# Remainders of the first difference tiles on GpSimd, and three more seven-product pairs, in an encoder layer

## The chip, the cores and the metric

The kernel runs on one core of one Trainium2 chip. The metric is the time of one execution in device microseconds; a time is a median over runs. The engines are named as in the profile: PE is TensorE (matmuls), DVE is VectorE, ACT is ScalarE, POOL is GpSimd, SP issues most DMAs.

## The reference

One layer of a bidirectional encoder in float32, for 256 tokens of width 4096:

```
h    = rms_norm(x, g_mix)
proj = h @ w_in                      # 4096 -> 11840: q, kv latents, rotary key, gates, dilated q, k, v
y_a  = rms_norm(mla_attention(...))     * silu(gate_a)      # 16 heads, latents through w_uq, w_ukv
y_b  = rms_norm(dilated_attention(...)) * silu(gate_b)      # 16 heads, three dilation patterns
x    = x + concat(y_a, y_b) @ w_out                          # 4096 -> 4096
gate = sigmoid(rms_norm(x, g_ple) @ w_ple_gate)              # 4096 -> 4096
x    = x + (p @ w_ple) * gate
out  = rms_norm(x, g_final)
```

Nearly all of the work is three large products: 256 x 4096 by 4096 x 11840, and twice 256 x 4096 by 4096 x 4096.

## The kernel before

**A product in three matmuls.** Every float32 operand is held as a high part in the fast float32 format and a remainder. ACT copies the source into `hi` (which rounds), and DVE subtracts: `lo = src - hi`. That is the helper `split`. A product `a b` is then three matmuls, `hi hi`, `hi lo`, `lo hi` (the helper `mm`). Each weight tile that is loaded must so be split before PE can use it; the left sides are split once.

**Blocks.** A `Block` computes 256 tokens by 1024 columns of one weight over a depth of 4096, which is 32 rows of tiles, called kt here. There are 18 of them: six dilated ones (`w_in`: q, k, v of heads 0 to 7, then of heads 8 to 15), five gate blocks (the first holds the q latent, the others `gate_b` and `gate_a`), three of `w_out`, four of `w_ple_gate` (the fourth leaves its last 8 kt to a closing part). Between them lie the kv latents, the attention heads and the half chunks of `w_out`, which have no pairs.

**Plain steps and pairs.** A plain step (`plain_step`) takes one kt: one load of 128x1024, one split of 128x1024 (ACT and DVE once each), four products of 128x512 (two token tiles by two column halves). A pair of kt can be done instead by a scheme of the Strassen kind with seven products for eight (`fast_steps`, kind "f" in the order of steps). It needs sums of the left side, made once by DVE (`add_sums`), and four differences of weight tiles, which DVE makes for each pair: `T[0]` (two of 128x512: the first difference tiles) and, from it, `T[1]`. A pair is four steps: "M1" (a half split, one product), "M2 M3" (a split of the second raw tile, two products), "M5 M7" (a split of `T[0]`, two products) and "M6 M4" (a split of `T[1]`, two products). So a pair costs DVE four differences of 128x512, one remainder of 128x512 and three of 128x1024.

**How many pairs.** Tables of numbers set the pairs in each block: `FAST_QKV`, `FAST_G`, `FAST_O`, `FAST_P`. The function `spread` lays the steps of a block out: some plain steps ahead (`LEAD_...`), some behind, and between them pairs and plain steps mixed by the DVE cost that a table gives each step:

```
FAST_COST, PLAIN_COST, PLAIN_TIME = (1.8, 2.3, 1.15, 1.15), 1.15, 2.73
FAST_TIME = 0.69, 1.37, 1.37, 1.37
```

At a block's end DVE adds the eight PSUM banks into the block's result: `d_mid` and `d_done` in the dilated blocks, with 11 instructions of 128x512 that read PSUM, and `gate_mid`, `gate_done`, `out_mid`, `out_done`, `wide_mid`, `wide_done` elsewhere.

**What sets the order.** Every engine runs its instructions in the order in which the program emits them. The emitter keeps a clock of its own for each engine (`Clock`, with a cost for each kind of instruction in `Metered`) and decides by it: it converts steps (loads, splits) ahead of the product that PE is at, up to five steps, and puts conversions ahead of other work when less than `MARGIN = 4.0` us are in hand. GpSimd's cost there is

```
us = n * 0.0024 + 0.1
```

for n elements a row, and each engine's cost is taken by itself. GpSimd's own work before is the 30 sums `acc += junk` of attention (128x256, both inputs in SBUF), four DMAs and some memsets.

Of the kernel before, what the change touches and what calls it, by code (L numbers as in the profile page):

```python
# [15 lines left out]
AF = mybir.ActivationFunctionType  # L16
ALU = mybir.AluOpType
# [3 lines left out]
S = 256  # L21
# [189 lines left out]
def encoder_layer(ctx: ExitStack, tc: tile.TileContext, x, p, positions, g_mix, w_in, g_q_latent, w_uq,  # L211
# [3 lines left out]
    nc = Engines(whole, clock)  # L215
# [11 lines left out]
    def slot(tag, shape, dtype=F32):  # L227
        names[tag] = names.get(tag, 0) + 1
        return clock.made(sp.tile([P, *shape], dtype, tag=tag, name=f"{tag}_{names[tag]}"), tag)

    def bank(tag, shape, bufs=1):
        names[tag] = names.get(tag, 0) + 1
        return clock.made(pp.tile([P, *shape], F32, tag=tag, name=f"{tag}_{names[tag]}", bufs=bufs), tag, bufs)
# [8 lines left out]
    def plain(t):  # L242
        return t.bitcast(F32)

    def split(hi, lo, src, scale=None):

        if scale is None:
            nc.scalar.activation(hi, src, AF.Copy)
            nc.vector.tensor_tensor(lo, src, plain(hi), op=ALU.subtract)
        else:  # L250
            nc.scalar.activation(hi, src, AF.Copy, scale=scale)
            nc.vector.scalar_tensor_tensor(lo, src, scale, plain(hi), op0=ALU.mult, op1=ALU.subtract)
# [10 lines left out]
    def mm(ps, a, b, start, stop):  # L263

        (ah, al), (bh, bl) = a, b
        nc.tensor.matmul(ps, ah, bh, start=start, stop=False)
        nc.tensor.matmul(ps, ah, bl, start=False, stop=False)
        nc.tensor.matmul(ps, al, bh, start=False, stop=stop)
# [883 lines left out]
    class Block:  # L1152
# [62 lines left out]
        def fast_steps(self, j):  # L1215

            r, T = [], []
            (A11, A21), (A12, A22) = [[lambda k=k, t=t: tuple(q[:, t * P:(t + 1) * P] for q in self.lhs(k))
                                       for t in range(NT)] for k in (2 * j, 2 * j + 1)]
            S = lambda n: (lambda: self.sums[j][n])  # L1220

            def sub(dst, a, b):
                nc.vector.tensor_tensor(dst, a, b, op=ALU.subtract)

            def split1(hi, lo):
                if isinstance(self.tmp, tuple):
                    T.extend(slot(b, [2, self.q]) for b in self.tmp)
                else:
                    both = slot(self.tmp, [4, self.q])
                    T.extend((both[:, :2], both[:, 2:]))  # L1230
                sub(T[0][:, 0], r[0][:, 1], r[0][:, 0])
                sub(T[0][:, 1], r[0][:, 1], r[1][:, 1])
                split(hi[:, 0], lo[:, 0], r[0][:, 0])

            def split2(hi, lo):
                nc.scalar.activation(hi, r[1], AF.Copy)
                sub(T[1][:, 0], r[1][:, 1], T[0][:, 0])
                sub(T[1][:, 1], r[1][:, 0], T[1][:, 0])
                nc.vector.tensor_tensor(lo, r[1], plain(hi), op=ALU.subtract)

            def run(*which):
                def go(hi, lo):
                    for i, (m, a) in enumerate(which):
                        self.product(m, a(), (hi[:, i], lo[:, i]))
                return go

            needs = [*self.needs(2 * j), *self.needs(2 * j + 1), (self.name, j), *self.fast_needs]
            more = [*needs, *self.turn_needs]
            return [
                self.step("M1", tuple(lambda k=k: r.append(self.load(k)) for k in (2 * j, 2 * j + 1)), split1, run(("M1", A11)), needs, 1, 0.69),  # L1250
                self.step("M2 M3", None, split2, run(("M2", A12), ("M3", S(3))), needs, 1, 1.37),
                self.step("M5 M7", None, lambda hi, lo: split(hi, lo, T[0]), run(("M5", S(0)), ("M7", S(2))), more, 0, 1.37),
                self.step("M6 M4", None, lambda hi, lo: split(hi, lo, T[1]), run(("M6", S(1)), ("M4", A22)), more, 0, 1.37),
            ]

# [94 lines left out]
    pT, ple, gF, U = [], {}, [], []  # L1350
    part2 = [[stat(1) for _ in range(4)] for _ in range(NT)]
    FAST, WIDE, LAST_K = 7, 4, 8
    FAST_P, LEAD_P, TRAIL_P = (7, 7, 7, 5), (6, 6, 6, 4), (4, 4, 4, 4)
    HALVES = (0, S), (S, Q)
    PLE_AT = 0, 3
    HURRY, REST, QUIET = -4, 0, 3
# [334 lines left out]
    G_BANKS = "m2", "m3", "s", "o", "m0", "m1", "t0", "t1"  # L1691
    H_BANKS = "m0", "m1", "t0", "t1", "m2", "m3", "s", "o"
    Y_BANKS = "s", "o", "t0", "t1", "m0", "m1", "m2", "m3"
    FAST_QKV, LEAD_QKV = (3, 7, 8, 8, 8, 7), (18, 4, 4, 4, 4, 4)
    FAST_G, LEAD_G = (3, 6, 7, 7, 7), (15, 10, 6, 6, 4)
    LEAD_L = LEAD_G[0]
    E_BANKS = "m2", "m3", "m0", "m1", "s", "o", "t0", "t1"
# [60 lines left out]
    for n, (dil, half) in enumerate(((None, 0), (1, 0), (1, 1), (0, 0), (0, 1))):  # L1758
        hook(len(steps), only(*(("t0", "t1"), ("m0", "m1"))[n % 2]))
        order = spread(FAST_G[n], LEAD_G[n], 4)  # L1760
        lo = {None: 0, 0: OFF_GA, 1: OFF_GB}[dil] + 1024 * half
# [120 lines left out]
    def tick():  # L1882

        advance(spare=slack(ran[0] + 1) > MARGIN)
# [4 lines left out]
    class Old(Step):  # L1889
# [18 lines left out]
        def run(self, hi, lo):  # L1908
            ch, j = self.ch, self.j
            if j == 0:  # L1910
                ch.ps = {t: bank(ch.banks[t], [512]) for t in ch.ts}
                locks.update(self.banks)
            for k in range(ch.per):
                kt = ch.per * j + k
                a = ch.lhs(kt)
                for t in ch.ts:
                    mm(ch.ps[t][:, :ch.n], tuple(q[:, t * P:(t + 1) * P] for q in a), (hi[:, k], lo[:, k]),
                       kt == 0, kt == ch.nk - 1)
                    tick()
            if ch.per * (j + 1) == ch.nk:  # L1920
                self.after = lambda: ch.done(Sums({t: q[:, :ch.n] for t, q in ch.ps.items()}, ch.banks))
# [156 lines left out]
```

## Time and profile before

| | before |
|---|---|
| time, median of 3 runs (lowest, highest) | 1900.3 us (1899.37, 1900.38) |
| the profiled execution | 1899.12 us, span 1897.4 us |
| granted TensorE clock | 0.998 |
| PE busy | 1878.5 us, 99% |
| DVE busy | 1696.8 us, 89% |
| ACT busy | 1140.2 us, 60% |
| POOL busy | 31.2 us, 2% |
| read from HBM | 364.72 MB, 194 GB/s over the span |

Busy is the time in which an engine has at least one instruction under way. In the profile's rows a line is nearly always L177, that of the helper through which every instruction is emitted; the tiles tell what a row is. `lo<-T,hi` or `B<-T,B` is a remainder of a difference tile (the tiles that hold splits change: `hi` and `lo`, `B`, `T`, `B7a` and `B7b`, `Ah`, `Al`); `lo<-raw,hi` is one of a loaded tile; `T<-raw,T` a difference. Digits of buffers are left out.

### The profile page before, as it was taken

How to read it: one execution, taken by the hardware profiler on the slowest of the kernel's cores; microseconds unless marked ns; L12 is line 12 of the kernel's file. 1: busy time of each engine (PE TensorE's matmuls, PEld its weight loads, DVE VectorE, ACT ScalarE, POOL GpSimd, SP SyncE). 2: the span in 40 equal slices, each digit the busy share in tenths (PEclk: the TensorE clock that was granted, in tenths of full speed). 3: DMA queues.
4: the chain of work that ended last, by engine and by line, in shares of the span. 5: the costliest groups of instructions: out<-in, count | busy, mean ns of one | idle time of the engine just before them, and what ended most of it. 6: DMA issues, size and time to landing. Idle time of an engine off the chain costs nothing.

```text
span 1897.4 us, 25417 instructions
## 1 busy us (share of the span) xinstructions
PE 1878.5 (99%) x9133; PEld 1579.8 (83%) x9133; DVE 1696.8 (89%) x2354; ACT 1140.2 (60%) x1543; POOL 31.2 (2%) x41
## 2 busy tenths in 40 slices
PE   9999999999999999999999999999999999999997
PEld 7888888888899888888888999888888888888885
DVE  6999999899898989999998777999989989989897
ACT  7655656565588555556556556656655555666654
POOL 0000000000011000000000010100000000000000
PEclk9999999999999999999999999999999999999999
DMA  8666666666735566666667553576666666665665
GB/s 279 189 205 213 214 212 200 198 213 193 218 84 159 166 211 183 196 215 189 208 199 209 137 142 123 167 231 204 216 199 217 187 194 218 194 223 183 221 222 180
DMA packets 160871, 370.59 MB, mean 195 GB/s; under 512 B 29116, under 2 KB 70952, under 8 KB 160744
## 3 DMA queue, kind: packets, MB, share of 16 engines
q1 hardware_dynamic: 159896, 366.58, 62.0%
q0 software_dynamic: 512, 1.84, 0.3%
q8 instruction: 72, 1.18, 0.3%
q10 hardware_dynamic: 336, 0.54, 0.1%
q14 instruction: 55, 0.45, 0.1%
HBM read 364.72 MB, written 4.19 MB: 194 GB/s over the span
## 4 chain that ended last, share of the span: by engine, by line
PE 85%; DVE 10%; DMA 2%; issue 2%; ACT 1%; POOL 0%; DVEq 0%; ACTq 0%; POOLq 0%
PE m L177 49%; PE t L177 16%; PE s L177 11%; PE o L177 9%; DVE lo L177 3%; DVE B L177 3%; DVE T L177 2%; DVE Ah L177 1%; DMA raw<-in_w_ple_gate_dram 1%; DVE Al L177 1%; DMA raw<-in_w_in_dram 1%; ACT hi L177 0%; DVE st L177 0%; ACT B L177 0%; DVE B7b L177 0%
## 5 line engine op out<-in xcount | busy, mean ns | idle before, releaser
L177 ACT ACTIVATE hi<-raw 128x1024 fp32r<-128x1024 f32 (+2 forms) x396 | 378.9, 966 | 278.1 <-PE m L177 70.9
L177 DVE TENSOR_TENSOR lo<-raw,hi 128x1024 fp32r<-128x1024 f32 (+2 forms) x396 | 433.4, 1107 | 61.8 <-ACT hi L177 60.6
L177 PE MATMUL m<-hi,Ah 128*128 128x512 f32 (+2 forms) x659 | 247.2, 387 | 0.3 <-ACT hi L177 0.3
L177 DVE TENSOR_TENSOR B<-raw,B 128x1024 fp32r<-128x1024 f32 (+3 forms) x228 | 213.9, 947 | 20.5 <-ACT B L177 18.8
L177 PE MATMUL m<-hi,Al 128*128 128x512 f32 (+2 forms) x625 | 229.6, 380 | 0.0
L177 PE MATMUL m<-lo,Ah 128*128 128x512 f32 (+2 forms) x549 | 207.8, 379 | 1.4 <-DVE lo L177 1.3
L177 ACT ACTIVATE B<-raw 128x1024 fp32r<-128x1024 f32 (+2 forms) x142 | 135.3, 962 | 96.8 <-DMA raw<-in_w_in_dram 25.3
L177 PE MATMUL m<-hi,B 128*128 128x512 f32 (+1 forms) x524 | 179.0, 389 | 0.0
L177 PE MATMUL m<-B,Ah 128*128 128x512 f32 (+2 forms) x554 | 146.7, 359 | 0.6 <-DVE B7b L177 0.6
L177 PEld LDWEIGHTS m<-hi,Ah 128*128 128x128 f32 x659 | 124.0, 188 | 22.7 <-ACT hi L177 1.2
L177 PEld LDWEIGHTS m<-hi,Al 128*128 128x128 f32 x625 | 117.5, 188 | 21.8
L177 PEld LDWEIGHTS m<-lo,Ah 128*128 128x128 f32 x549 | 103.4, 188 | 19.9 <-DVE lo L177 2.9
L177 PEld LDWEIGHTS m<-hi,B 128*128 128x128 f32 x524 | 98.2, 188 | 19.6
L177 PEld LDWEIGHTS m<-B,Ah 128*128 128x128 f32 x554 | 95.9, 189 | 15.3 <-DVE B7b L177 1.0
L177 PE MATMUL m<-lo,B 128*128 128x512 f32 (+1 forms) x262 | 102.1, 390 | 0.1
L177 PE MATMUL m<-B,Al 128*128 128x512 f32 (+2 forms) x289 | 99.1, 371 | 0.0
L177 DVE TENSOR_TENSOR T<-raw,T 128x512 f32<-128x512 f32 (+2 forms) x110 | 85.5, 789 | 3.3 <-ACT T L177 1.7
L177 ACT ACTIVATE hi<-B 128x1024 fp32r<-128x1024 f32 x57 | 59.4, 1056 | 23.1 <-PE m L177 7.3
L177 DVE TENSOR_TENSOR lo<-B,hi 128x1024 fp32r<-128x1024 f32 x57 | 68.5, 1220 | 3.9 <-ACT hi L177 3.6
L177 PE MATMUL t<-hi,Ah 128*128 128x512 f32 x184 | 69.9, 391 | 0.0
L177 ACT ACTIVATE B<-T 128x1024 fp32r<-128x1024 f32 (+2 forms) x55 | 50.2, 916 | 22.8 <-DVE T L177 13.4
L177 PEld LDWEIGHTS m<-B,Al 128*128 128x128 f32 x289 | 54.4, 188 | 9.2
(530 smaller groups left out, 4336.9 us busy)
## 6 DMA issues: line engine op xcount, KB each, us to landing
raw<-in_w_in_dram SPq DMA_DIRECT2D x359, 512.0 KB, 4.3
raw<-in_w_out_dram SPq DMA_DIRECT2D x128, 512.0 KB, 4.6
raw<-in_w_ple_gate_dram SPq DMA_DIRECT2D x128, 512.0 KB, 4.7
raw_q<-in_w_uq_dram SPq DMA_DIRECT2D x32, 256.0 KB, 3.8
T<-in_x_dram SPq DMA_DIRECT2D x13, 512.0 KB, 6.6
raw<-in_w_in_dram SPq DMA_DIRECT2D x16, 320.0 KB, 3.1
raw_r<-in_w_uq_dram SPq DMA_DIRECT2D x16, 256.0 KB, 4.3
raw_k<-in_w_ukv_dram SPq DMA_DIRECT2D x16, 256.0 KB, 3.4
```

The source lines that it names most:

```text
L177: return do(out, *rest, **named)
```

## The change

In the step "M5 M7" of every pair, the remainder `T[0] - hi` moves from DVE to GpSimd; ACT's copy stays. Three blocks get one pair more: the second and the sixth dilated block (7 to 8), and the fourth `w_ple_gate` block (5 to 6). There were 116 pairs, and there are 119. The cost tables of `spread` stay.

```diff
+            def split3(hi, lo):
+                nc.scalar.activation(hi, T[0], AF.Copy)
+                nc.gpsimd.tensor_tensor(lo, T[0], plain(hi), op=ALU.subtract)
+
...
-                self.step("M5 M7", None, lambda hi, lo: split(hi, lo, T[0]), run(("M5", S(0)), ("M7", S(2))), more, 0, 1.37),
+                self.step("M5 M7", None, split3, run(("M5", S(0)), ("M7", S(2))), more, 0, 1.37),
...
-    FAST_P, LEAD_P, TRAIL_P = (7, 7, 7, 5), (6, 6, 6, 4), (4, 4, 4, 4)
+    FAST_P, LEAD_P, TRAIL_P = (7, 7, 7, 6), (6, 6, 6, 4), (4, 4, 4, 4)
...
-    FAST_QKV, LEAD_QKV = (3, 7, 8, 8, 8, 7), (18, 4, 4, 4, 4, 4)
+    FAST_QKV, LEAD_QKV = (3, 8, 8, 8, 8, 8), (18, 4, 4, 4, 4, 4)
```

In the third dilated block one pair stands on DVE like this before. `T_23_2677` is its first difference tile, `T_24_2678` its second, `raw_2641` and `raw_2643` the two loaded tiles; `B_12_2706` is the remainder of a plain step that lies between:

```order
L177 TENSOR_TENSOR T_23_2677<-raw_2641 128x512
L177 TENSOR_TENSOR T_23_2677<-raw_2641,raw_2643 128x512
L177 TENSOR_TENSOR B_21_2676<-raw_2641,B_21_2676 128x512
L177 TENSOR_TENSOR T_24_2678<-raw_2643,T_23_2677 128x512
L177 TENSOR_TENSOR T_24_2678<-raw_2643,T_24_2678 128x512
L177 TENSOR_TENSOR B_21_2689<-raw_2643,B_21_2689 128x1024
L177 TENSOR_TENSOR B_12_2706<-raw_2662,B_12_2706 128x1024
L177 TENSOR_TENSOR lo_2720<-T_23_2677,hi_2719 128x1024
L177 TENSOR_TENSOR T_18_2732<-T_24_2678,T_18_2731 128x1024
```

The last row but one is the remainder of the first difference tile. A pair of the same block on DVE in the changed kernel (`T_23_2605` and `T_24_2606` are its difference tiles, `T_17_2626` and `B_14_2646` remainders of plain steps):

```order
L177 TENSOR_TENSOR T_23_2605<-raw_2575 128x512
L177 TENSOR_TENSOR T_23_2605<-raw_2575,raw_2577 128x512
L177 TENSOR_TENSOR B_20_2604<-raw_2575,B_20_2604 128x512
L177 TENSOR_TENSOR T_17_2626<-raw_2589,T_17_2625 128x1024
L177 TENSOR_TENSOR T_24_2606<-raw_2577,T_23_2605 128x512
L177 TENSOR_TENSOR T_24_2606<-raw_2577,T_24_2606 128x512
L177 TENSOR_TENSOR B_20_2635<-raw_2577,B_20_2635 128x1024
L177 TENSOR_TENSOR B_14_2646<-raw_2611,B_14_2646 128x1024
L177 TENSOR_TENSOR lo_2667<-T_24_2606,hi_2666 128x1024
```

No remainder of `T_23_2605` is left there; the row with `T_24_2606` follows at once. It stands on POOL, among those of the pairs around it:

```order
L177 TENSOR_TENSOR B_19_2522<-T_21_2476,B_19_2522 128x1024
L177 TENSOR_TENSOR lo_2586<-T_22_2542,hi_2585 128x1024
L177 TENSOR_TENSOR lo_2660<-T_23_2605,hi_2659 128x1024
L177 TENSOR_TENSOR B_21_2729<-T_24_2686,B_21_2729 128x1024
L177 TENSOR_TENSOR B_22_2792<-T_25_2748,B_22_2792 128x1024
```

POOL has one such row for each pair, one behind the other, and nothing between them in the blocks. PE reads the result in the products M5 and M7 of that pair:

```order
L177 MATMUL m_4_2514<-hi_2659,B_1_580 128x512
L177 MATMUL m_4_2514<-lo_2660,B_1_580 128x512
L177 MATMUL m_4_2514<-hi_2659,B_1_580 128x512
L177 MATMUL m_4_2518<-hi_2659,B_1_580 128x512
L177 MATMUL m_4_2518<-lo_2660,B_1_580 128x512
L177 MATMUL m_4_2518<-hi_2659,B_1_580 128x512
```

The order on PE is as before; what changes is that `lo_2660` is waited for from GpSimd.

## Prediction

> **What bounds the kernel now.** I read the page first, then the waits of PE, then the busy time of each engine block by block, and last the timeline of DVE and POOL where the two work at once.
>
> ```profile
> span 1897.4 us, 25417 instructions
> PE 1878.5 (99%) x9133; PEld 1579.8 (83%) x9133; DVE 1696.8 (89%) x2354; ACT 1140.2 (60%) x1543; POOL 31.2 (2%) x41
> PE m L177 <- DVE junk L177: 1.5, 1, 1.5
> PE m L177 <- DVE lo L177: 1.3, 3, 0.8
> ```
>
> PE is busy 99% of the span and its two longest sums of waits are 1.5 and 1.3 us: TensorE sets the time and hardly ever waits. DVE stands at 89%, second, and POOL at 2%. The next view decides the case. It gives the busy times in the 18 blocks that hold seven-product pairs; each stretch begins where a block's first product starts. In order: six dilated blocks, five gate blocks (the first is the q latent), three output blocks, four w_ple_gate blocks (the last without its closing part).
>
> ```profile
> core 0: us, PE busy (x) PEld busy (x) DVE busy (x) ACT busy (x) POOL busy (x), PEclk, DMA share, GB/s
> 6.10:100.40 94.30, 93.42 (x437) 76.39 (x438) 82.45 (x147) 65.09 (x113) 0.00 (x0) 1.00 0.72 239
> 100.40:183.10 82.70, 82.66 (x365) 67.95 (x364) 79.94 (x106) 48.20 (x57) 0.00 (x0) 1.00 0.66 205
> 183.10:265.60 82.50, 81.89 (x362) 67.48 (x361) 80.24 (x95) 46.39 (x51) 0.00 (x0) 1.00 0.66 212
> 265.60:347.20 81.60, 81.60 (x362) 67.57 (x361) 76.36 (x89) 47.67 (x50) 0.00 (x0) 1.00 0.64 206
> 347.20:428.80 81.60, 81.60 (x362) 67.57 (x361) 75.87 (x89) 47.62 (x49) 0.00 (x0) 1.00 0.66 206
> 428.80:511.10 82.30, 82.30 (x365) 68.15 (x364) 75.18 (x86) 47.31 (x49) 0.69 (x1) 1.00 0.70 216
> ...
> 594.90:686.50 91.60, 91.56 (x431) 76.06 (x431) 81.88 (x153) 54.32 (x85) 4.34 (x4) 1.00 0.59 184
> 686.50:771.40 84.90, 84.90 (x384) 70.28 (x383) 75.42 (x105) 50.05 (x62) 0.00 (x0) 1.00 0.65 194
> 771.40:855.50 84.10, 84.10 (x380) 69.68 (x379) 77.83 (x95) 50.20 (x55) 0.00 (x0) 1.00 0.66 206
> 855.50:939.70 84.20, 84.20 (x381) 69.72 (x381) 77.81 (x95) 50.44 (x55) 0.00 (x0) 1.00 0.66 200
> 939.70:1022.00 82.30, 82.30 (x365) 68.15 (x364) 73.96 (x86) 46.77 (x50) 0.00 (x0) 1.00 0.67 195
> ...
> 1226.50:1310.20 83.70, 83.42 (x369) 68.52 (x368) 78.71 (x103) 46.15 (x52) 0.00 (x0) 1.00 0.67 220
> 1310.20:1394.70 84.50, 84.46 (x381) 69.66 (x380) 78.12 (x96) 50.35 (x62) 0.00 (x0) 1.00 0.66 210
> 1394.70:1480.50 85.80, 85.51 (x383) 70.01 (x382) 75.46 (x91) 48.76 (x61) 0.72 (x1) 1.00 0.67 216
> ...
> 1527.50:1614.10 86.60, 86.57 (x385) 70.92 (x384) 77.22 (x100) 49.87 (x59) 0.00 (x0) 1.00 0.66 206
> 1614.10:1699.10 85.00, 85.00 (x377) 70.38 (x376) 79.13 (x92) 52.99 (x63) 0.00 (x0) 1.00 0.64 209
> 1699.10:1784.10 85.00, 85.00 (x377) 70.38 (x376) 77.99 (x91) 52.06 (x62) 0.00 (x0) 1.00 0.64 201
> 1784.10:1846.60 62.50, 62.19 (x275) 51.17 (x274) 57.53 (x74) 38.02 (x48) 0.00 (x0) 1.00 0.67 212
> ```
>
> In these blocks DVE is idle only 2 to 10 us of some 84: 82.50 - 80.24 = 2.3 us in the third dilated block, 2.8 in the second, 5 to 7 in the next three. That spare is all that added DVE time can go into before PE waits. One PE product is three matmuls; 81.60 us / 362 = 0.225 us each, so 0.68 us a product.
>
> **What each part costs.** *The three added pairs.* Each pair computes seven products in place of eight: 3 x 0.68 = 2.0 us less on PE in all, if PE is what is late there.
>
> *The moved subtraction.* It leaves DVE. The start-to-start times of DVE in a full stretch:
>
> ```profile
> 290.70 1.22 DVE L177 TENSOR_TENSOR lo<-raw,hi 128x1024 fp32r<-128x1024 f32 x1
> 291.84 1.22 DVE L177 TENSOR_TENSOR lo<-T,hi 128x1024 fp32r<-128x1024 f32 x1
> 294.11 0.68 DVE L177 TENSOR_TENSOR T<-raw 128x512 f32<-128x512 f32 x1
> 294.71 0.68 DVE L177 TENSOR_TENSOR T<-raw,raw 128x512 f32<-128x512 f32 x1
> ```
>
> A 128x1024 remainder takes 291.84 - 290.70 = 1.14 us of DVE (the reported 1.22 overlaps the next one), a 128x512 one 294.71 - 294.11 = 0.60. So each of the 116 pairs that were there gives DVE back 1.14 us.
>
> *What it adds.* POOL runs 119 subtractions of 128x1024 with both inputs in SBUF. Before shows POOL with two SBUF inputs only in the 128x256 sums of attention, among them these, beside DVE:
>
> ```profile
> L177 POOL TENSOR_TENSOR acc<-acc,junk x30: 732/745/1772, 535.6 to 1200.9; 128x256 f32<-128x256 f32 x30
> 608.77 1.77 POOL L177 TENSOR_TENSOR acc<-acc,junk 128x256 f32<-128x256 f32 x1 [8.33 <-ACT junk L177]
> 608.73 1.22 DVE L177 TENSOR_TENSOR B<-raw,B 128x1024 fp32r<-128x1024 f32 x1
> 609.87 0.70 DVE L177 SCALAR_TENSOR_TENSOR st<-st 128x2 f32<-128x2 f32 x1
> 610.80 0.16 DVE L177 SCALAR_TENSOR_TENSOR st<-st 128x2 f32<-128x2 f32 x1
> 535.64 0.73 POOL L177 TENSOR_TENSOR acc<-acc,junk 128x256 f32<-128x256 f32 x1 [42.56 <-ACT junk L177]
> 535.88 1.17 DVE L177 TENSOR_TENSOR lo<-raw,hi 128x640 fp32r<-128x640 f32 x1
> L177 DVE TENSOR_TENSOR lo<-raw,hi 128x640 fp32r<-128x640 f32 x10 | 8.5, 855 | 1.4 <-ACT hi L177 1.4
> 587.94 0.73 POOL L177 TENSOR_TENSOR acc<-acc,junk 128x256 f32<-128x256 f32 x1 [8.13 <-ACT junk L177]
> 588.32 0.69 DVE L177 TENSOR_TENSOR T<-t,T 128x512 fp32r<-128x512 f32 x1 [0.34 <-ACT T L177]
> ```
>
> Read them as three encounters. At 608.77 POOL starts just after a DVE subtraction and takes 1.77 us instead of 0.73: it stood still until DVE was done. The DVE instruction behind, on two numbers a row, then takes 0.70 instead of 0.16: DVE lost 0.54 us to POOL. At 535.88 POOL came first, and DVE's 128x640 remainder took 1.17 against a mean of 0.855: 0.32 lost, and it had begun 0.24 after POOL, 0.56 together. At 588.32 DVE read a transposed PSUM bank and only one SBUF tile: 0.69, nothing lost. So while POOL reads two SBUF tiles, DVE does no work that reads two SBUF tiles, and the other way round, whole instructions at a time. Nearly all of DVE's work in the blocks is of that kind. The Trainium skill's page "SBUF — State Buffer", section "Who interferes with whom", states that as an exclusive lock held for the whole instruction; the trace agrees on the lock, but shows 0.54 lost of 0.73.
>
> The price at 128x1024 isn't shown, and the smallest POOL instruction bounds what of it may be fixed:
>
> ```profile
> L177 POOL MEMSET ones<- 128x1 f32 x1 | 0.1, 100 | 0.0
> ```
>
> Bounds: 4 x 0.54 = 2.16 us if the lock goes with the elements; 0.10 fixed and 4 x 0.44, 1.86 together, as the low end; the whole instruction, 4 x 0.73 = 2.93, as the high one. I take 2.16, by the measured loss itself. The page "GPSIMD Engine Reference" of the Trainium skill, section "Elementwise — side-by-side cycle accounting", has 2.6 cycles an element at 1.2 GHz, an estimate of 2.22 us here; the sum below would be 5 us higher by it.
>
> So each moved remainder costs DVE 2.16 - 1.14 = +1.02 us net, though DVE "does less". An added pair costs DVE four differences and one half remainder (5 x 0.60), two full remainders (2.28) and the lock (2.16), and spares two plain remainders (2.28): +5.16.
>
> *The sum, block by block.* New DVE time = the row's DVE busy + 1.02 for each pair there (8, 8, 8 and so on by the pair tables) + 5.16 where a pair is added, + 0.6: the 2.3 us that DVE leaves idle even in its fullest block, less what runs under the locks. That is the eleven PSUM-reading additions of a block,
>
> ```profile
> L177 DVE SCALAR_TENSOR_TENSOR B<-m,st,B 128x512 f32<-128x512 f32 x26 | 17.8, 742 | 0.1
> ```
>
> 8 us, of which the share under locks (8 x 2.16 of 82 us, 21%) is 1.7. What exceeds the stretch's old length is added time.
>
> - Dilated, second (7 pairs, one added): 79.9 + 7.1 + 5.2 + 0.6 = 92.8, over 82.7 by 10.1. Third (8): 89.0, +6.5. Fourth: 85.1, +3.5. Fifth: 84.6, +3.0. Sixth (7, one added): 88.1, +5.8. First (3): 86.1, under 94.3.
> - Gates (3, 6, 7, 7, 7): the third and fourth 85.6, +1.5 and +1.4; the others fit.
> - Output (6, 7, 6): +1.7, +1.4, fits.
> - w_ple_gate (7, 7, 7, 5 and one added): fits, +1.9, +0.7, and 57.5 + 5.1 + 5.2 + 0.6 = 68.4, +5.9.
>
> Together +43 us. The three products saved on PE are worth nothing: all three lie in blocks where DVE is late. The six blocks that fit keep 8.2, 6.1, 2.8, 0.6, 3.6 and 1.6 us spare, 23 together; the pairs stand close within a block, so some of that spare comes at the wrong time. Bounds 0 and 23; I take a third, +8. The remainder itself arrives later for PE: up to 1.14 of waiting and 2.2 to 2.9 of work instead of 1.2. The look-ahead of the conversions, kept at 4.0 us by the planner, hides that; if it is used up by DVE's lag, the wait is the same one already counted. Kv, heads, the half chunks and the end hold no pairs: nothing. ACT at 60% and the DMA queue keep their work.
>
> Sum: 1899.1 (the profiled execution, span 1897.4 and 1.7 around it) + 43 + 8 = 1950; the median shown is 1.2 above that execution, so 1952 us, +2.7%.
>
> **The rivals.** *The lock does not grow with the size* (not slower). If POOL holds DVE off for some 0.54 us at 128x1024 too and for the rest only slows itself, each pair frees 0.60 us of DVE. Then PE alone counts: 2.0 us of products and the 0.65 us that it stood still in the second and third dilated blocks: 1896.5, or 1898 beside the median, -0.14%. It decides from a lock of about 0.8 us (second dilated block: 79.9 + 3.0 + 0.6 + 8 locks - 8.0 = 82.0) and 1.3 us (third). For it: the rows show one size alone. Against: the two loss figures are most of POOL's own 0.73, so the lock follows its reading.
>
> *The whole instruction is locked*, at 2.93 us: 0.77 more for each of the 90 pairs in the full blocks, +69, and four of the six others spill, +12: 1899 + 43 + 81 = 2023, or 2024. Against: 0.54 of 0.73. The lock rule of the Trainium skill's page "SBUF — State Buffer" (section "Who interferes with whom") would give this.
>
> *No spare can be used*: DVE's lag hits PE at once, in tight handovers such as transposes that wait for DVE. 116 x 1.02 + 3 x 5.16 - 2 = 132: 2031, or 2032. Against: the look-ahead.
>
> **How the numbers follow.** Forecast 0.80, fixed lock 0.07, whole-instruction lock 0.07, no spare 0.06. The low end is the forecast with a lock of 1.86 and no unevenness: the same sums then give 7.7 + 4.1 + 1.1 + 0.6 + 3.4 + 4.1 = 21: 1920. The high end is half-way from 1952 to the dearer two at 2032: 1992. A change of 0.2% (3.8 us) is about what a measurement of this kernel can tell from none. Slower by over that: 0.93; the fixed lock lies mostly within it, 0.05; faster 0.02.
>
> **What would show it.** Right: POOL remainders of 2.2 to 2.9 us, longer where they met DVE; DVE's 128x1024 remainders spread from 1.2 to over 3 us, with DVE busy above 1800 us although it holds fewer instructions; PE idle in the dilated blocks, released by lo tiles, the second worst; no change from kv to the heads. Wrong: POOL at 2.2 us with DVE's remainders still at 1.22; PE still at 99%; or PE's waits alike in blocks with three pairs and with eight.

## The result and the profile after

The changed kernel takes 2022.8 us (median of 6 runs) against 1899.2 before; the ratio is 1.0647, 95% interval [1.0634, 1.0661]. It is slower, as forecast, but by 124 us where 52 were forecast, and outside the range of 1920 to 1992. One of the six executions took 8.1 ms with PE slow throughout, and it was the one profiled; so all lines of the changed kernel below come from a second profiled execution of the same file, 2020.4 us, span 2018.4.

The head of its page, and the longest waits of PE in it (in total, times, longest):

```profile
span 2018.4 us, 25470 instructions
PE 1907.3 (94%) x9124; PEld 1575.9 (78%) x9124; DVE 1806.9 (90%) x2253; ACT 1143.1 (57%) x1549; POOL 356.8 (18%) x160
PE m L177 <- DVE lo L177: 39.8, 33, 3.0
PE s L177 <- DVE B L177: 17.4, 16, 1.6
PE s L177 <- DVE lo L177: 11.0, 9, 2.1
```

PE fell from 99% to 94% busy and waits for DVE's tiles, remainders above all; GpSimd's remainders are not what it waits for. DVE holds about 100 instructions fewer and is busy 110 us longer (1696.8 before). The line to look at is what is left: DVE's idle time was 1897.4 - 1696.8 = 200.6 us, and is 2018.4 - 1806.9 = 211.5. In total it did not shrink.

Busy time by block, columns as before: the first five dilated blocks, the first three gate blocks, the heads, and the first w_ple_gate block.

```profile
6.00:105.50 99.50, 94.80 (x436) 75.94 (x437) 87.58 (x152) 66.47 (x115) 8.25 (x3) 1.00 0.68 224
105.50:199.20 93.70, 85.69 (x362) 68.10 (x361) 92.46 (x98) 49.09 (x58) 22.22 (x8) 0.98 0.60 188
199.20:285.60 86.40, 83.05 (x361) 67.14 (x360) 85.14 (x82) 46.19 (x50) 23.36 (x8) 1.00 0.62 196
285.60:372.80 87.20, 83.17 (x361) 67.18 (x361) 85.34 (x82) 46.20 (x50) 22.56 (x8) 1.00 0.61 192
372.80:460.20 87.40, 82.84 (x361) 67.19 (x361) 84.11 (x82) 46.74 (x50) 21.86 (x8) 1.00 0.62 193
...
636.00:732.50 96.50, 92.63 (x430) 75.76 (x430) 84.88 (x150) 54.08 (x85) 12.66 (x7) 1.00 0.57 174
732.50:823.90 91.40, 86.15 (x384) 69.98 (x383) 80.14 (x99) 49.99 (x62) 15.25 (x6) 1.00 0.61 182
823.90:914.60 90.70, 85.63 (x380) 69.28 (x379) 83.44 (x88) 50.00 (x55) 18.71 (x7) 1.00 0.62 191
...
1092.80:1237.30 144.50, 144.50 (x1035) 135.89 (x1034) 109.36 (x174) 86.37 (x164) 8.94 (x9) 1.00 0.53 147
...
1616.00:1711.20 95.20, 87.91 (x384) 70.54 (x383) 85.00 (x94) 51.21 (x60) 18.96 (x7) 1.00 0.59 193
```

The second dilated block went from 82.7 to 93.7, about as summed (+11.0, where +10.1 was forecast). But the second gate block, which should have fitted, went from 84.9 to 91.4 while DVE idled 11 of 91 us; the first w_ple_gate block, which should have fitted too, from 86.6 to 95.2 with 10 us idle. The two blocks with only three pairs, the first dilated and the first gate block, lost 5 us each, though the sum had 8 and 6 us of spare there. Of the blocks with pairs, DVE's idle time shrank only in the second to fifth dilated one, from 16.0 to 7.6 us together. Where there are no pairs nothing changed: the heads took 144.5 us before as well.

The lock looks as foretold. One encounter, POOL and DVE, in the fourth dilated block:

```profile
304.73 2.81 POOL L177 TENSOR_TENSOR B<-T,B 128x1024 fp32r<-128x1024 f32 x1 [7.82 <-ACT B L177]
305.19 3.44 DVE L177 TENSOR_TENSOR lo<-raw,hi 128x1024 fp32r<-128x1024 f32 x1
```

DVE's remainder takes 3.44 us in place of 1.22: 2.22 lost to one GpSimd remainder. On average over all 119 it is less, worked out from DVE's busy time: 110.1 us more, although 116 x 1.14 = 132.2 went away and the added pairs brought some 3 x 3.0 = 9.0 without the lock. That makes (110.1 + 132.2 - 9.0) / 119 = 1.96 us a lock.

### The profile page after: what moved, and what is told of

The parts are those of the page before. It is cut to its first block, busy times and chain, and to the rows that moved or that the text cites. A ratio compares the mean times of both kernels' runs of the same rounds, so it can differ in the third digit from the quotient of the medians.

```text
span 8119.0 us, 25470 instructions
## 1 busy us (share of the span) xinstructions
PE 8104.6 (100%) x9124; PEld 5156.0 (64%) x9124; DVE 1638.4 (20%) x2253; ACT 1178.0 (15%) x1549; POOL 305.4 (4%) x160
## 4 chain that ended last, share of the span: by engine, by line
PE 100%; DVE 0%; ACT 0%; issue 0%; DVEq 0%
PE m L177 57%; PE t L177 20%; PE s L177 13%; PE o L177 10%; DVE T L177 0%; DVE st L177 0%; DVE Ah L177 0%; ACT Ah L177 0%; DVE junk L177 0%; DVEq L2078 0%; ACT gT L177 0%
## 5 line engine op out<-in xcount | busy, mean ns | idle before, releaser
L177 PE MATMUL m<-hi,Ah 128*128 128x512 f32 (+2 forms) x669 | 862.0, 1309 | 0.0
L177 PE MATMUL m<-hi,Al 128*128 128x512 f32 (+2 forms) x637 | 810.6, 1293 | 0.0
L177 PE MATMUL m<-lo,Ah 128*128 128x512 f32 (+2 forms) x558 | 736.8, 1320 | 0.0
L177 PE MATMUL m<-B,Ah 128*128 128x512 f32 (+2 forms) x534 | 598.6, 1307 | 0.0
L177 PE MATMUL m<-hi,B 128*128 128x512 f32 (+1 forms) x544 | 586.7, 1160 | 0.0
L177 PEld LDWEIGHTS m<-hi,Ah 128*128 128x128 f32 x669 | 421.0, 629 | 226.1 <-issue 216.7
L177 PEld LDWEIGHTS m<-hi,Al 128*128 128x128 f32 x637 | 404.7, 635 | 223.5 <-issue 219.0
L177 PEld LDWEIGHTS m<-lo,Ah 128*128 128x128 f32 x558 | 374.2, 671 | 174.0 <-issue 169.7
L177 PEld LDWEIGHTS m<-B,Ah 128*128 128x128 f32 x534 | 380.6, 756 | 141.6 <-issue 140.3
L177 PE MATMUL m<-B,Al 128*128 128x512 f32 (+2 forms) x273 | 355.3, 1348 | 0.0
```

The costliest lines, as they stand in the source:

```text
L177: return do(out, *rest, **named)
```

## The experiments

**The changed kernel once more.**

> The changed kernel once more, for a trace of an ordinary execution: about 2021 us. All theories have GpSimd's remainder of 128x1024 at 2.35 us or more (its mean in the trace of the very long execution, in which PE was slow and DVE mostly idle). Lock with usable spare (the forecast's): DVE busy about 1820 us, PE idle in the overloaded blocks alone, nothing in blocks with three pairs. No usable spare: PE also idle in the blocks that the sum had as fitting (first dilated, first, second and fifth gate block, third output block, first w_ple_gate block), by about 1 us a pair everywhere. Late remainders: PE waits are put down to POOL, not to DVE.

This is the profile above. Waits are put down to DVE, which speaks against late GpSimd remainders as such; the six blocks that should have fitted lost about 1 us for each pair on average (from 0.5 to 1.7), which speaks for spare that can't be used. PE idles 4.7 us in the first dilated block, with three pairs, and 3.4 to 4.6 in the third to fifth, with eight: alike, which the prediction had named as a sign of being wrong.

**The move alone**: the changed kernel with the pair tables of before.

```diff
-    FAST_P, LEAD_P, TRAIL_P = (7, 7, 7, 6), (6, 6, 6, 4), (4, 4, 4, 4)
+    FAST_P, LEAD_P, TRAIL_P = (7, 7, 7, 5), (6, 6, 6, 4), (4, 4, 4, 4)
...
-    FAST_QKV, LEAD_QKV = (3, 8, 8, 8, 8, 8), (18, 4, 4, 4, 4, 4)
+    FAST_QKV, LEAD_QKV = (3, 7, 8, 8, 8, 7), (18, 4, 4, 4, 4, 4)
```

> The move alone: the pair tables of before, all 116 remainders on GpSimd. Usable spare: the forecast's sums without the added pairs give +5.0 and +0.6 in place of 10.1 and 5.8, +0.7 in place of 5.9, so 1899 + 28 + 8 = 1935 us. No usable spare: 116 x 1.02 to 1.21 = +118 to +140, 2017 to 2039 us; the measured +123.6 with 15 for the added pairs would leave about +108, 2007 us.

2008.2 us against 1898.4, ratio 1.0577 [1.056, 1.0595]: +110 us, 0.95 us a pair. The forecast's way of counting gave 1935. In the profiled execution, span 2005.8, DVE is busy 1791.7 us, 94.9 more than before, and idle 214.1 us, 13.5 more.

**The pairs alone**: the kernel before with the changed tables, `split` on DVE as it was.

> The three pairs alone, all remainders on DVE. Usable spare: DVE gets 4.1 us more in each of three blocks and PE 0.68 less; the second dilated block spills by 2.0, the other two fit and gain 0.68 each: 1899.8 us. No usable spare: 3 x 4.1 = +12, 1911 us.

1908.3 us, ratio 1.0048 [1.0033, 1.0063]: +9.9 us, near the 12 of "no spare". Computing three products fewer on PE costs time even without GpSimd, where DVE is busy 11.7 us more (1708.5). So 110 of the 124 us belong to the move, 10 to the pairs, and the rest to both together.

**No reading by GpSimd**: the changed kernel with

```diff
-                nc.gpsimd.tensor_tensor(lo, T[0], plain(hi), op=ALU.subtract)
+                nc.gpsimd.memset(plain(lo), 0.0)
+                nc.gpsimd.memset(plain(lo), 0.0)
```

> The changed kernel with GpSimd's subtraction replaced by two memsets of the same tile (the remainders of the first difference tiles are zero): GpSimd reads nothing from SBUF, DVE has the same instructions as in the changed kernel. Lock theories, with or without spare: the whole loss goes, 1896 to 1898 us. If the loss came from something else of the new order or the added pairs, 1910 us or more stay.

1896.4 us, ratio 0.9988 [0.9978, 0.9997]: all of the loss is gone, and the gain of 2.0 us is what the saved products were said to be worth. The largest groups of POOL and DVE in its trace:

```profile
L177 POOL MEMSET lo<- 128x1024 f32 x130 | 124.2, 955 | 672.4 <-PE t L177 228.3 <-PE m L177 197.5 <-PE o L177 168.8
L177 DVE TENSOR_TENSOR lo<-raw,hi 128x1024 fp32r<-128x1024 f32 x305 | 369.0, 1220 | 75.3 <-ACT hi L177 72.5 <-issue 1.7
```

Two memsets are 1.9 us of GpSimd a pair, and DVE's remainders stay at 1.220. So neither the new order nor busy time on GpSimd costs the time; what is left is that GpSimd reads SBUF. DVE is busy 1583.9 us here, 113 less than before, so that the added pairs fit. (The memsets need not wait for ACT, so this says nothing on remainders that reach PE late; the run with two pieces below does.)

**Half a tile.** The move alone, with

```diff
-                nc.gpsimd.tensor_tensor(lo, T[0], plain(hi), op=ALU.subtract)
+                nc.gpsimd.tensor_tensor(lo[:, 0], T[0][:, 0], plain(hi)[:, 0], op=ALU.subtract)
+                nc.gpsimd.memset(plain(lo)[:, 1], 0.0)
```

> The move alone (pair tables of before), but GpSimd subtracts only the first 128x512 half of each first difference tile; the second half of the remainder is set to zero by a GpSimd memset. A lock that goes with the elements: GpSimd holds DVE off for half of 2.2 us, as long as DVE is relieved (1.14), so about 1898 to 1903 us. A lock of fixed length: as with the whole tile, 2008 us.

1911.7 us, ratio 1.0065 [1.0049, 1.0082]: +13 where the whole tile costs +110. The lock goes with the elements; a fixed one, the first rival, falls. But the result lies above the 1898 to 1903 expected: DVE is busy 1645.2 us, 52 less than before, and still 13 us are lost. That part does not come from DVE's total work, and its cause stays open.

**Two pieces** of 128x512 in place of one instruction:

```diff
-                nc.gpsimd.tensor_tensor(lo, T[0], plain(hi), op=ALU.subtract)
+                for c in range(2):
+                    nc.gpsimd.tensor_tensor(lo[:, c], T[0][:, c], plain(hi)[:, c], op=ALU.subtract)
```

> The move alone, each remainder as two GpSimd instructions of 128x512 in place of one of 128x1024. If DVE's total time counts (pair stretch full before, every held-off microsecond paid): 2006 to 2015 us, as with one. If it's the length of one blocking (a single stop of 2.3 us that the look-ahead can't cover): clearly less, 1940 to 1985 us.

1991.3 us, ratio 1.0485 [1.0469, 1.05]: +93, between the two expectations. Cutting the remainder in two is worth some 17 of the 110 us; most of the loss stays when the same total is cut. GpSimd's rows, the changed kernel's first and these second:

```profile
L177 POOL TENSOR_TENSOR lo<-B,hi 128x1024 fp32r<-128x1024 f32 x24 | 65.9, 2744 | 269.7 <-ACT hi L177 269.7
L177 POOL TENSOR_TENSOR lo<-B,hi 128x512 fp32r<-128x512 f32 x48 | 88.7, 1869 | 244.3 <-ACT hi L177 204.6 <-DVE T L177 39.6
```

Two pieces take 2 x 1.87 = 3.7 us where the whole took 2.74, so the whole remainder is ready later, and yet less is lost. That speaks against late remainders as the cause.

**Room between the pairs.** Where is the spare that the sum counted on? The third gate block before and after (the same block, cut in 10 us from its start; DVE busy is the fourth column of times):

```profile
771.40:781.40 10.00, 10.00 (x46) 8.29 (x45) 8.25 (x12) 6.85 (x10) 0.00 (x0) 1.00 0.61 189
781.40:791.40 10.00, 10.00 (x54) 8.29 (x53) 9.95 (x17) 6.11 (x9) 0.00 (x0) 1.00 0.70 207
791.40:801.40 10.00, 10.00 (x46) 8.29 (x45) 9.18 (x11) 5.58 (x6) 0.00 (x0) 1.00 0.65 199
801.40:811.40 10.00, 10.00 (x46) 8.28 (x45) 9.76 (x13) 5.47 (x8) 0.00 (x0) 1.00 0.68 208
811.40:821.40 10.00, 10.00 (x46) 8.29 (x45) 9.93 (x12) 6.86 (x7) 0.00 (x0) 1.00 0.53 163
821.40:831.40 10.00, 10.00 (x46) 8.29 (x45) 9.90 (x13) 6.82 (x8) 0.00 (x0) 1.00 0.69 215
831.40:841.40 10.00, 10.00 (x46) 8.28 (x45) 9.22 (x11) 4.57 (x6) 0.00 (x0) 1.00 0.73 218
841.40:855.50 14.10, 14.10 (x64) 11.68 (x63) 11.63 (x12) 7.94 (x9) 0.00 (x0) 1.00 0.69 235
```

```profile
853.90:863.90 10.00, 10.00 (x45) 8.03 (x43) 9.70 (x8) 5.43 (x7) 4.18 (x2) 1.00 0.56 194
863.90:873.90 10.00, 8.65 (x37) 6.79 (x37) 9.80 (x10) 5.05 (x6) 2.44 (x1) 1.00 0.52 157
873.90:883.90 10.00, 8.74 (x38) 6.87 (x37) 9.71 (x10) 5.57 (x7) 2.56 (x1) 1.00 0.59 168
883.90:893.90 10.00, 8.91 (x40) 7.05 (x38) 9.87 (x10) 5.58 (x6) 3.35 (x1) 1.00 0.65 206
893.90:903.90 10.00, 8.62 (x38) 6.84 (x37) 9.62 (x9) 4.96 (x5) 2.58 (x1) 1.00 0.54 159
903.90:914.60 10.70, 10.70 (x49) 8.85 (x48) 8.33 (x10) 4.86 (x6) 0.00 (x0) 1.00 0.83 270
```

Before, the 6.3 us in which DVE idles lie mostly at the block's two ends (1.75 in the first 10 us, 2.5 in the last 14); from 801 to 831, among the pairs, DVE is 97.6 to 99% busy and PE still never waits. After, from 864 to 904, PE loses 1.1 to 1.4 us in each 10, and has its full pace again at the end, where no pair stands.

Most of the other blocks are alike. The trace of the move alone tells at which matmuls the first and the last of a block's GpSimd remainders fall. In the trace of before, DVE idles 35 us between those matmuls, over all 18 blocks, of 124 us in the whole of the blocks. The stretch of the pairs before in the first and fourth dilated and in the first w_ple_gate block:

```profile
65.50:86.00 20.50, 20.50 (x92) 16.91 (x91) 19.98 (x44) 9.74 (x11) 0.00 (x0) 1.00 0.60 189
274.70:336.80 62.10, 62.10 (x276) 51.42 (x275) 59.25 (x68) 37.17 (x39) 0.00 (x0) 1.00 0.64 204
1547.20:1597.40 50.20, 50.17 (x220) 40.79 (x219) 49.12 (x64) 28.57 (x32) 0.00 (x0) 1.00 0.64 201
```

DVE is 97 to 98% busy in the first and the third of them. In the first dilated block only 0.5 of its 11.8 idle us lie among the pairs; in the fourth 2.9 of 5.2 do.

To test it, fewer plain steps at the ends and more between the pairs, first in the kernel before, with all remainders on DVE:

```diff
-    FAST_P, LEAD_P, TRAIL_P = (7, 7, 7, 5), (6, 6, 6, 4), (4, 4, 4, 4)
+    FAST_P, LEAD_P, TRAIL_P = (7, 7, 7, 5), (3, 3, 3, 2), (2, 2, 2, 4)
...
-    FAST_QKV, LEAD_QKV = (3, 7, 8, 8, 8, 7), (18, 4, 4, 4, 4, 4)
+    FAST_QKV, LEAD_QKV = (3, 7, 8, 8, 8, 7), (18, 2, 2, 2, 2, 2)
-    FAST_G, LEAD_G = (3, 6, 7, 7, 7), (15, 10, 6, 6, 4)
+    FAST_G, LEAD_G = (3, 6, 7, 7, 7), (15, 8, 3, 3, 2)
...
-    FAST_O, LEAD_O = (6, 7, 6), (4, 5, 4)
+    FAST_O, LEAD_O = (6, 7, 6), (3, 3, 3)
```

and the steps behind the pairs from 2 to 1 in the dilated blocks, from 4 to 2 in the gate and output blocks.

> The kernel before, with fewer plain steps ahead of and behind the pairs of a block and so more of them between the pairs (remainders on DVE, same pair tables). Both theories: PE is late nearly everywhere and stays so, 1896 to 1900 us; up to 1910 if the steps taken away at the ends were needed for the sums or the banks.

1935.1 us, ratio 1.0191 [1.0176, 1.0206]: a miss. The plain steps at the ends are needed in some of the blocks; what for was not shown. Then the same layout with the move:

> The move alone, with the same wider layout. Theory that DVE is already full in the stretch of the pairs and its spare lies at the two ends of a block: each plain step that comes between the pairs brings 2.73 us of PE against 1.14 of DVE, 1.6 us of spare; three to five steps a block are 5 to 8 us against 6 to 8 us of added DVE time, so most of the 110 us goes: 1915 to 1950 us. Theory that DVE's lag always hits PE through tight handovers, wherever the spare is: 2000 to 2015 us.

1990.4 us, ratio 1.048 [1.0464, 1.0495]. On its own layout the move costs 1990.4 - 1935.1 = 55 us, half of 110. As a total that decides neither way. Block by block it does, where the layout alone costs nothing. The second and third w_ple_gate block, in three kernels: the move alone, the wide layout, the wide layout with the move.

```profile
1703.20:1794.80 91.60, 86.54 (x376) 69.99 (x375) 83.98 (x85) 51.95 (x61) 18.55 (x7) 1.00 0.59 191
1794.80:1886.40 91.60, 86.56 (x377) 70.00 (x376) 83.46 (x84) 52.19 (x62) 18.43 (x7) 1.00 0.58 186
```

```profile
1644.80:1730.40 85.60, 85.31 (x377) 70.32 (x376) 78.61 (x92) 52.02 (x61) 0.00 (x0) 1.00 0.63 202
1730.40:1815.40 85.00, 85.00 (x377) 70.38 (x376) 76.69 (x89) 52.21 (x62) 0.00 (x0) 1.00 0.63 199
```

```profile
1695.60:1782.40 86.80, 85.52 (x376) 70.20 (x375) 83.84 (x84) 50.42 (x61) 21.38 (x7) 1.00 0.61 198
1782.40:1868.60 86.20, 85.43 (x377) 70.35 (x377) 82.40 (x82) 52.00 (x62) 21.11 (x7) 1.00 0.60 197
```

Both blocks take 85.0 before and 91.6 with the move. With five plain steps more among the pairs the move costs 1.2 us in each instead of 6.6, and DVE idles 3 to 4 us instead of 8. The same seven GpSimd remainders are there. The second gate block, with four steps more, agrees: 84.9 before, 91.3 with the move, 84.9 in the wide layout, 85.3 with both. Nor is the lag passed on: the fourth w_ple_gate block behind them takes 69.2 us in the wide layout and 70.0 with both. So it is the place of the spare that decides, not a handover that no spare can help. It is shown for these blocks; in the dilated blocks the layout put only three steps more among the pairs, and much of the loss stayed.

**The planner told the price.** The move alone, with

```diff
         self.free[engine] = at + us
+        if engine == "pool" and us > 2:
+            self.free["dve"] += 2.2
...
-    FAST_COST, PLAIN_COST, PLAIN_TIME = (1.8, 2.3, 1.15, 1.15), 1.15, 2.73
+    FAST_COST, PLAIN_COST, PLAIN_TIME = (1.8, 2.3, 2.2, 1.15), 1.15, 2.73
```

> The move alone, with the planner told the price: 2.2 us in the cost table for the M5 M7 step, and 2.2 us of DVE charged for each GpSimd remainder. If the loss comes from an order that was planned for a DVE that is freer than it is: most of it goes, 1930 to 1960 us. If DVE has no room in the stretch of the pairs, whatever the order there: 1990 to 2012 us.

1996.4 us, ratio 1.0512 [1.0494, 1.0529]: +98. An order made with a cost near the measured one saves 12 of 110 us; the steps at a block's ends stay where they are.

**Every second pair.** The move alone, with

```diff
             def split3(hi, lo):
+                if j % 2:
+                    return split(hi, lo, T[0])
```

> The move alone in every second pair (the even ones of a block, 61 of 116; the others keep DVE). Stretch of the pairs full from the first remainder on: the loss goes with the number, 61 of 116 of +110 = +58, 1956 us. A spare that has to be used up first: clearly under half, 1905 to 1930 us.

1948.1 us, ratio 1.0261 [1.0245, 1.0276]: +49. The trace holds 64 such remainders, not 61; 64 of 116 by 110 would be 61 us. In total it is nearly proportional: some 11 us less, where the forecast's way of counting had 118 - 36 = 82 us of the whole move vanish in spare. Block by block it is not. The fourth dilated, the third gate and the first w_ple_gate block, with four remainders on GpSimd in each:

```profile
273.40:355.00 81.60, 81.60 (x362) 67.57 (x360) 80.45 (x87) 47.28 (x50) 11.64 (x4) 1.00 0.66 207
787.80:874.90 87.10, 84.76 (x380) 69.55 (x379) 80.52 (x91) 49.88 (x55) 10.74 (x4) 1.00 0.64 198
1560.80:1653.30 92.50, 87.35 (x385) 70.81 (x384) 81.86 (x97) 50.84 (x60) 11.19 (x4) 1.00 0.62 198
```

The dilated block takes 81.6 us as before, and DVE's idle time there goes from 5.2 to 1.2: its spare was used. The other two lose 3.0 and 5.9 us, and DVE stays idle for 6.6 and 10.6 us of them, most of it at the blocks' ends.

**One input in place of two.** The move alone, with two GpSimd copies of the high part in place of the subtraction.

> The move alone, with each subtraction replaced by two GpSimd copies of the high part into the remainder (the remainders of the first difference tiles are so wrong by that): GpSimd reads one SBUF tile an instruction, not two. If any GpSimd instruction that reads SBUF holds off DVE's two-input instructions: about as long as the copies take, DVE's remainders up to 2 us and more, and with some 2 us a pair 1980 to 2010 us. If only GpSimd's two-input instructions do: DVE at 1.22 throughout, 1897 to 1900 us.

1939.1 us (one run), +40, between the two expectations. POOL and DVE in its trace:

```profile
307.00 3.71 POOL L177 CAST T<-T 128x1024 fp32r<-128x1024 f32 x2 [6.79 <-ACT T L177]
307.74 2.06 DVE L177 TENSOR_TENSOR B<-raw,B 128x1024 fp32r<-128x1024 f32 x1
309.73 2.05 DVE L177 TENSOR_TENSOR B<-T,B 128x1024 fp32r<-128x1024 f32 x1
```

Each copy costs DVE 2.06 - 1.22 = 0.84 us. GpSimd holds DVE off with one input as well, for less time, while the memsets, which only write, left DVE's rows at 1.220. So it is the reading that locks.

## Why the prediction was wrong

*What held.* The direction; the lock, "whole instructions at a time"; its price, 2.16 us taken, 2.22 measured in the encounter shown and 1.96 on average; that it goes with the elements; that PE is released by DVE's tiles and not by GpSimd's, and that the second is the worst of the dilated blocks; no change where no pairs stand. DVE's added time was summed as 116 x 1.02 + 3 x 5.16 = 134 us; it came out as 110 us more busy, since the average lock is 0.2 us shorter.

*The step that failed* is the next one: "What exceeds the stretch's old length is added time", with DVE's idle time of a whole block as spare. It gave +43, and +8 for unevenness with a bound of 23. The idle time was real, but most of it lay at the ends of the blocks, in plain steps, out of reach of the pairs (35 of 124 us lay among them): the blocks that should have fitted lost 3 to 9 us each, and DVE's total idle time did not shrink. The term for unevenness was where this belonged; at 8, and even at its bound of 23, it was far too small. The look-ahead that was named as the cover does not carry it over: in the third gate block PE was already losing 1.35 us in the second 10 us of the stretch shown after. A view in 10 us slices of one block, made of the trace of before, would have shown 97 to 99% there. The added pairs beside the move were priced about right: 15 of the 43 us, and 124 - 110 = 14 were measured; alone, with all remainders on DVE, the same counting gave +0.6, where +9.9 was measured.

*The rivals.* "No spare can be used" gave 2032 and was right to 10 us, but was given 0.06. Its reason, tight handovers, is not what the blocks of the wide layout show; there the spare could be used once it stood among the pairs. "The whole instruction is locked" gave 2024, the measured time, by luck. Its mechanism is nearly right: GpSimd's remainder takes 2.35 us on average in the execution of 8.1 ms, where DVE was 20% busy, and 2.22 of that were lost. But its sum needs 2.93 us, four times the small instruction, and the usable spare that was not there. (It counts 90 pairs in the full blocks; the tables give 87, and its time would be 2 us lower.) "The lock does not grow" fell with the half tile.

*Left open*: the 4 us by which both parts together cost more than each alone; the 13 us of the half tile; and some 11 us of the move's 110 that are neither DVE's added busy time (94.9) nor the clock, below (some 4).

## What to carry to other kernels

An engine's spare counts only in the stretch in which the new work falls: cut the trace finer than the block, look at the slices that hold the work, and ask whether that engine is idle there. Work that GpSimd reads from SBUF is not work taken off DVE while DVE streams two SBUF inputs: here 1.14 us were saved for 2.0 to 2.2 us of standing still, and the busy shares (DVE 89%, POOL 2%) showed none of it; the few encounters in the trace did.

## What was not expected of the hardware

A short stop of PE can be followed by a stretch at half its clock. In the first output block of the changed kernel, PE's starts around a wait, and the two stretches behind it:

```profile
1315.14 0.39 PE L177 MATMUL m<-B7a,Ah 128*128 128x512 f32 x1
1317.52 0.50 PE L177 MATMUL m<-B7b,Ah 128*128 128x512 f32 x1 [1.98 <-DVE B7b L177]
...
1318.50:1321.90 3.40, 3.40 (x9) 2.63 (x9) 3.31 (x6) 0.16 (x1) 0.00 (x0) 0.50 0.81 260
1321.90:1328.70 6.80, 6.80 (x31) 5.58 (x31) 6.25 (x6) 5.44 (x6) 2.38 (x1) 1.00 0.81 276
```

After a wait of 1.98 us the granted clock is 0.50 for 3.4 us, with 9 matmuls where 15 would have started at 0.225 us each, some 1.4 us more on top of the wait. The Trainium skill, "TensorE: Matmul & The Clock Gate", section "What's actually happening", has the half clock after an idle window of about 3.4 us; here the wait was shorter than that. Not every stop does it: behind its first 5 us this trace has eight gaps of 2.4 to 3.4 us between matmul starts, and four of them are followed by such a stretch; no shorter gap is. Leaving out the last 10 us, the move alone has three such stretches and the kernel before none, so the clock is some 3 x 1.4 = 4 of the 110 us, an estimate.

In the kernel with the pairs alone, the second dilated block has such a stretch too, behind a wait of 2.17 us for a tile from ACT, which had waited for DVE:

```profile
170.00:177.30 7.30, 7.09 (x20) 5.64 (x21) 7.20 (x13) 4.35 (x5) 0.00 (x0) 0.62 0.55 153
```

20 matmuls in 7.3 us where 32 would go: 2.7 us of that kernel's 9.9, the waits among them included.
